# Joint buffers for the two fp16 halves of a row: one transpose of 2048 columns for two of 1024, and one load for both rotary tables

## The chip, the cores and the metric

The kernel runs on one core of one Trainium2 chip. The metric is device time in microseconds (us); the kernel before took 1997.04 us, the median of three runs. Engines are called as in the profile: PE (matmul), PEld (its weight load), DVE, ACT, POOL, and SP, which in this kernel does no arithmetic and issues every DMA, the transposes among them.

## The reference

Two layers of a hybrid encoder on a sequence of 2048 tokens of width 1024, then a final norm. Cut to what matters:

```python
def hybrid_layer(x, norm_gain, w_in, w_out, rel_bias, cos, sin):
    hn = rms_norm(x, norm_gain)
    aq, ak, av, ag, rq, rk, rv, rg = split(hn @ w_in)        # eight parts of 512 columns
    ya = chunked_rel_attention(aq, ak, av, rel_bias)         # 8 heads of 64, own chunk of 64 + 8 before
    yr = chunkwise_retention(rq, rk, rv, cos, sin)           # 4 heads of 128, rotary phases, group norm
    y = concatenate([ya * silu(ag), yr * silu(rg)])          # 2048 x 1024
    return x + y @ w_out
def reference(x, ...):
    for layer in range(2): x = hybrid_layer(x, ...)
    return rms_norm(x, final_gain)
```

## The kernel before

**Number format.** Products run on PE in fp16. Each f32 operand is split into an upper half (rounded to fp16) and a lower half (the rest, in fp16), and a product is the sum of three: upper by upper, upper by lower, lower by upper. So everything that goes to PE exists twice, as `...h` and `...l`.

**Tiling.** 128 rows of tokens are a token tile; there are 16, t = 0 to 15. Four token tiles make a stretch n of 512 tokens. A layer has four sections s, each with its share of the attention and retention heads. The normed input of a layer, turned so that the width lies on the partitions, is kept in `hTh` and `hTl`, one pair a stretch, 8 blocks of 128 rows by 512 tokens each.

**Within a section and stretch.** `dense_T` (product at L758) and `dense_V` (L778) make q, k, v and gates from `hTh`/`hTl` and the weights `whT`/`wlT`, `whV`/`wlV`. `dense_T` loads the rotary tables `tabc` and `tabs` (cosine and sine, 256 KB each, L638 and L639), which POOL multiplies into q and k of the retention (L695, L696). Attention goes unit by unit: PE makes the scores `S` (L826, L827), DVE adds the bias and takes the maximum into `sc` (L830), ACT takes the exponential in place (L833) and writes its upper half into `pq` (L835), POOL writes the lower half behind it (L836), SP turns `pq` into `pT` by one DMA transpose (L838), and PE multiplies by v (L848, L849). `sc`, `pq` and `pT` have two buffers each.

**At a layer's end** the rows of y, which sections stored to `y_d`, go through W_out, a token tile at a time. For tile t: load y (`yyy`, L959), squares on ACT (L981), a scale, the upper half on ACT (L236, `rows_hi`), the lower half on DVE (L242, `rows_lo`), and two transposes of 1024 columns on SP (L246, `transpose_rows`, called by `y_turn`) into `yhy` and `yly`; PE then does 48 matmuls of 512 columns with W_out's `whO` and `wlO` (L1115), in the order upper by upper, upper by `wlO`, lower by upper; DVE adds x; x is stored (L1123). At layer 0's end x of the tile is also normed at once for layer 1 (`residual`): squares, root, product with the gain (L1024), upper half on ACT (L236), lower half on DVE (L240), two transposes (L246) into `hTh` and `hTl` of layer 1.

**Where rows lie.** A row pair is a place for 128 rows of 1024 columns, upper and lower. At layer 0's end tiles 0 to 7 of y use room in `hTl`/`hTh` of a stretch that is not needed yet (so `yhy<-hTl` in the profile is a turn of y), the residual of tiles 0 to 3 uses the weight buffers `whT` and `wlT`, and the others take attention's `sc` (upper) and `pq` (lower): `rhy`, `rly` for y, `rhn`, `rln` for the residual. At layer 1's end all of y uses `hTh`/`hTl`. The turned y uses the buffers `tabc`, `tabs` for even t, `qq`, `swp` for odd t, `pT` for t = 15.

**What sets the order.** On PE, ACT, DVE and POOL the order is that of the program; at the layers' ends two tables of step names (`LAYER`, `LAST`) say in which round of PE's work each step stands (`yh7` is the upper half of tile 7's y, `nl4` the lower half of tile 4's residual, `nx4` its transposes, `yt7` the turn of y). SP's order is found by a scheduler, except for some DMAs that are held in the program's order. A DMA waits on SP until its sources and its target are free, and whatever stands behind it in SP's queue waits too.

Of the kernel before, what the change touches and what calls it, by code (L numbers as in the profile page):

```python
# [18 lines left out]
P = 128  # L19
# [8 lines left out]
def hybrid_trunk(ctx: ExitStack, tc: tile.TileContext, x, pos, gain, gcol, w_in, w_out, rel, fgain,  # L28
# [180 lines left out]
    hT = {}  # L209
    ring = {}  # L210
# [13 lines left out]
    def hT_of(l, n):  # L224
        if (l, n) not in hT:
            hT[l, n] = (hp.tile([P, KT, 512], F16, tag="hTh", name=f"hTh{l}_{n}"),
                        hp.tile([P, KT, 512], F16, tag="hTl", name=f"hTl{l}_{n}"))
        return hT[l, n]

    def row_pair(nm):  # L230
        return (b2.tile([P, 1280], F16, tag="sc", name=f"rh{nm}")[:, 0:D],
                b2.tile([P, 1280], F16, tag="pq", name=f"rl{nm}")[:, 0:D])

    def rows_hi(rows, xt, s_=None):

        act.activation(rows[0], xt, AF.Copy, scale=1.0 if s_ is None else s_[:, 0:1])  # L236

    def rows_lo(rows, xt, s_=None):
        if s_ is None:
            dve.tensor_tensor(rows[1], xt, rows[0], op=ALU.subtract)  # L240
        else:
            dve.scalar_tensor_tensor(out=rows[1], in0=xt, scalar=s_[:, 0:1], in1=rows[0], op0=ALU.mult, op1=ALU.subtract)  # L242

    def transpose_rows(rows, dh, dl, turn=False):
        for d, r in ((dh, rows[0]), (dl, rows[1])):
            i = sp.dma_start_transpose(out=d, in_=r)  # L246
            if turn:
                in_turn(i)

    class Tok:  # L250
# [46 lines left out]
        def dma(self):  # L297
            transpose_rows(self.rw, self.hh, self.hl)
# [330 lines left out]
    def dense_T(l, s, n, g, st):  # L629
        hh, hl = hT[l, n]  # L630
        nm = f"{l}_{s}_{n}"
        st.tabc = b1.tile([P, 512], F32, tag="tabc", name=f"tabc{nm}")
        st.tabs = b1.tile([P, 512], F32, tag="tabs", name=f"tabs{nm}")
        def tab_load():
            while n not in tab_done:
                assert bg
                pull(1)
            in_turn(sp.dma_start(st.tabc, tab_d[n][0]))  # L638
            in_turn(sp.dma_start(st.tabs, tab_d[n][1]))  # L639
# [164 lines left out]
    def attention(l, s, n, g, st, prev):  # L804
# [6 lines left out]
        def qk(a, hx):  # L811
# [16 lines left out]
            v = b2.tile([P, 640], F32, tag="sc", name=f"sc{u.nm}")[:, 0:w]  # L828
# [5 lines left out]
            pq = b2.tile([P, 1280], F16, tag="pq", name=f"pq{u.nm}")  # L834
# [139 lines left out]
    def y_squares(l, u):  # L974
        u.m = b2.tile([P, 1], F32, tag="ym", name=f"ym{u.nm}")
        if l + 1 == DEPTH or u.t < 8:
            f = (hT[l, 1] if l + 1 == DEPTH else hT_of(l + 1, NS - 2))[u.t // 2 % 2].rearrange("p k c -> p (k c)")
            u.rows = [f[:, (u.t % 2 * 2 + i) * D:(u.t % 2 * 2 + i + 1) * D] for i in range(2)]
        else:
            u.rows = row_pair(u.nm)  # L980
        act.activation(u.rows[0], u.y, AF.Square, accum_out=u.m)  # L981
# [28 lines left out]
    def residual(l, t, xt, rows):  # L1010

        hh, hl = (h_[:, :, t % 4 * P:(t % 4 + 1) * P] for h_ in hT_of(l, t // 4))
# [20 lines left out]
        for f, fn in (("q", sq), ("r", root), ("m", mul), ("u", upper), ("l", lower),  # L1033
                      ("x", lambda: transpose_rows(u.rows, hh, hl))):
# [27 lines left out]
    def wout(l, go, gc, us, wT=None):  # L1062
# [6 lines left out]
        for r in range(6 * NT):  # L1069
# [46 lines left out]
            if i % 3 == 2:  # L1116
# [59 lines left out]
    def norm_steps(ts, spaces, rows):  # L1176
# [495 lines left out]
```

## Time and profile before

| | |
|---|---|
| median of 3 runs | 1997.04 us (1996.8 to 1997.64) |
| the profiled execution: its time | 1997.53 us |
| its span, first to last instruction | 1995.8 us |
| PE busy | 1977.3 us (99%) |
| DVE, ACT, POOL busy | 1233.1, 1153.7, 699.2 us |
| granted clock of PE | 1.00 |
| DMA traffic | 316.08 MB, mean 158 GB/s |

Such rows are read thus. A timeline row has the start in us, the duration in us, the engine, the source line, the operation, output <- inputs, and in brackets how long the engine stood idle before it and what released it. SPq is SP's queue: the time that it took to issue, waits of the DMA for its sources included. In the view of a tile a row has the instructions' durations in ns as shortest, median and longest; the line "DMA to landing" has the time from the begin of the issue to the data's arrival as shortest, median and longest. In the view of waits a row has who waited, for whom, the total in us, how often, and the longest.

### The profile page before, as it was taken

How to read it: one execution, taken by the hardware profiler on the slowest of the kernel's cores; microseconds unless marked ns; L12 is line 12 of the kernel's file. 1: busy time of each engine (PE TensorE's matmuls, PEld its weight loads, DVE VectorE, ACT ScalarE, POOL GpSimd, SP SyncE). 2: the span in 40 equal slices, each digit the busy share in tenths (PEclk: the TensorE clock that was granted, in tenths of full speed). 3: DMA queues.
4: the chain of work that ended last, by engine and by line, in shares of the span. 5: the costliest groups of instructions: out<-in, count | busy, mean ns of one | idle time of the engine just before them, and what ended most of it. 6: DMA issues, size and time to landing. Idle time of an engine off the chain costs nothing.

```text
span 1995.8 us, 36717 instructions
## 1 busy us (share of the span) xinstructions
PE 1977.3 (99%) x12874; PEld 1039.7 (52%) x12874; DVE 1233.1 (62%) x3665; ACT 1153.7 (58%) x2523; POOL 699.2 (35%) x701
## 2 busy tenths in 40 slices
PE   8999999999999999999999999999999999999998
PEld 5455555555555555554445555555555555555544
DVE  8787756665556655676545556555655565567544
ACT  8667756465656545655445556565656565456432
POOL 1444343434434334420013444344333443343100
PEclk9999999999999999999999999999999999999999
DMA  8899566566655654999974556665566485568864
GB/s 248 189 189 198 145 140 145 131 141 137 143 126 145 145 121 117 217 235 265 266 161 108 105 122 136 144 146 110 138 151 150 104 180 125 122 126 190 234 200 137
DMA packets 657899, 316.08 MB, mean 158 GB/s; under 512 B 471569, under 2 KB 614417, under 8 KB 657714
## 3 DMA queue, kind: packets, MB, share of 16 engines
q1 hardware_dynamic: 657714, 313.75, 68.1%
q8 instruction: 100, 1.64, 0.4%
q14 instruction: 85, 0.70, 0.1%
HBM read 122.74 MB, written 41.98 MB: 83 GB/s over the span
## 4 chain that ended last, share of the span: by engine, by line
PE 94%; DMA 1%; DVE 1%; issue 0%; POOL 0%; ACT 0%; SPq 0%; POOLq 0%; ACTq 0%
PE dV L778 32%; PE dT L758 31%; PE dO L1115 16%; PE r L883 4%; PE o L848 3%; PE S L826 3%; PE S L827 3%; PE o L849 2%; DMA yly<-hTl 0%; DMA pT<-pq 0%; DVE hTl L1002 0%; DMA swp<-rot 0%; DVE hTh L1191 0%; DVE hTl L242 0%; POOL swp L696 0%
## 5 line engine op out<-in xcount | busy, mean ns | idle before, releaser
L836 POOL TENSOR_TENSOR pq<-sc,pq 128x640 f16<-128x640 f32 (+4 forms) x256 | 322.2, 1259 | 949.7 <-ACT pq L835 463.2
L833 ACT ACTIVATE sc<-sc,mq,cT 128x640 f32<-128x640 f32 (+4 forms) x256 | 218.3, 853 | 397.3 <-DVE mq L832 288.5
L778 PE MATMUL dV<-whV,hTh 128*128 128x512 f16 x1024 | 351.5, 379 | 0.0
L778 PE MATMUL dV<-wlV,hTh 128*128 128x512 f16 x1024 | 351.5, 379 | 0.0
L778 PE MATMUL dV<-whV,hTl 128*128 128x512 f16 x1024 | 351.5, 379 | 0.0
L758 PE MATMUL dT<-hTh,whT 128*128 128x512 f16 x992 | 340.5, 379 | 0.5 <-DVE xb L96 0.5
L758 PE MATMUL dT<-hTh,wlT 128*128 128x512 f16 x992 | 340.5, 379 | 0.0
L758 PE MATMUL dT<-hTl,whT 128*128 128x512 f16 x992 | 340.5, 379 | 0.0
L778 PEld LDWEIGHTS <-hTh 128*128 128x128 f16 x2048 | 195.9, 98 | 211.4
L758 PEld LDWEIGHTS <-whT 128*128 128x128 f16 x1984 | 189.0, 98 | 202.1 <-DVE hTl L290 1.0
L830 DVE CUSTOM_DVE_ANT_0 sc<-S,bias 128x640 f32<-128x640 f32 (+4 forms) x256 | 188.5, 736 | 134.2 <-PE S L827 133.2
L1115 PE MATMUL dO<-whO,yly 128*128 128x512 f16 x504 | 191.0, 379 | 1.9 <-DMA yly<-hTl 1.9
L1115 PE MATMUL dO<-whO,yhy 128*128 128x512 f16 x504 | 191.0, 379 | 0.0
L1115 PE MATMUL dO<-wlO,yhy 128*128 128x512 f16 x504 | 191.0, 379 | 0.0
L835 ACT ACTIVATE pq<-sc 128x640 f16<-128x640 f32 (+4 forms) x256 | 171.5, 670 | 8.1
L1115 PEld LDWEIGHTS <-yhy 128*128 128x128 f16 x1008 | 98.0, 98 | 113.7 <-issue 0.3
L778 PEld LDWEIGHTS <-hTl 128*128 128x128 f16 x1024 | 99.0, 98 | 110.1
L758 PEld LDWEIGHTS <-wlT 128*128 128x128 f16 x992 | 95.8, 98 | 106.2
L826 PE MATMUL S<-k,q 128*128 128x128 f16 (+3 forms) x592 | 142.4, 267 | 0.0
L848 PE MATMUL o<-v,pT 128*128 128x129 f16 x1120 | 132.4, 221 | 0.4 <-DMA pT<-pq 0.4
L827 PE MATMUL S<-k,q 128*128 128x128 f16 (+3 forms) x592 | 129.3, 266 | 0.0
L849 PE MATMUL o<-v,pT 128*128 128x65 f16 x1120 | 125.7, 193 | 0.0
(357 smaller groups left out, 3260.9 us busy)
## 6 DMA issues: line engine op xcount, KB each, us to landing
q<-qq SPq DMA_DIRECT2D x128, 128.0 KB, 2.4
yyy<-y_d SPq DMA_DIRECT2D x32, 512.0 KB, 4.5
stT<-in_w_in_dram SPq DMA_DIRECT2D x27, 512.0 KB, 5.0
stV<-in_w_in_dram SPq DMA_DIRECT2D x26, 512.0 KB, 4.5
k<-kk SPq DMA_DIRECT2D x128, 64.0 KB, 2.0
swp<-rot SPq DMA_DIRECT2D x64, 128.0 KB, 3.7
tabc<-tab SPq DMA_DIRECT2D x32, 256.0 KB, 2.9
tabs<-tab SPq DMA_DIRECT2D x32, 256.0 KB, 3.1
```

Source lines behind the costliest of these rows:

```text
L758: pe.matmul(ps, w_[:, j, kt, :], h_[:, kt, :], start=(m == 0), stop=(m == 23))
L778: pe.matmul(ps, h_[:, kt, a * P:(a + 1) * P], w_[:, kt, :], start=(m == 0), stop=(m == 23))
L826: pe.matmul(o, st.q[:, hx, 0, cs], k_, start=True, stop=False)
L827: pe.matmul(o, st.q[:, hx, 1, cs], k_, start=False, stop=True)
L830: dve.tensor_tensor_reduce(out=v, in0=S[:, 0:w], in1=g.bias[hx][:, 640 - w:640], scale=1.0, scalar=-3.0e38, op0=ALU.add, op1=ALU.max, accu ...
L833: act.activation(v, v, AF.Exp, bias=m[:, 0:1], scale=g.c[:, 0:1])
L835: act.activation(pq[:, 0:w], v, AF.Copy)
L836: pool.tensor_tensor(pq[:, w:2 * w], v, pq[:, 0:w], op=ALU.subtract)
L848: pe.matmul(o[:, u.hx, 0:129], u.p[:, b, :], v_, start=(b == 0), stop=False)
L849: pe.matmul(o[:, u.hx, 0:65], u.p[:, u.nb + b, :], v_[:, 0:65], start=False, stop=(b == u.nb - 1))
L883: pe.matmul(out_, w_, m_, start=(i == 0), stop=(i + 1 == len(pairs)))
L1115: pe.matmul(ps, h_[:, kt, :], w_[:, kt, :], start=(m == 0), stop=(m == 23))
```

## The change

The two halves of a row pair now lie side by side in one buffer, and so do the two halves of the turned result; where nothing else forbids it, one transpose of 2048 columns turns both.

- `hTh` and `hTl` become one tile `hT`, upper half first.
- `sc` (f32, 640 columns) and `pq` (fp16, 1280 columns) become one tile `sc` of 2560 fp16 columns with two buffers. Attention uses its first half for scores and its second for the fp16 halves. A row pair takes its first 2048 columns.
- `residual`'s transposes at layer 0's end: one of 2048 columns a tile. For t < 4 both halves lie in `wT.g.h` or both in `wT.g.l`.
- `y_turn`: even t by one transpose of 2048 columns into the tables' buffer, odd t still by two of 1024.
- The rotary tables become one tile `tab`, loaded by one DMA of 512 KB, 32 times in all.
- The transposes at layer 0's start stay in halves.

```diff
     def hT_of(l, n):
         if (l, n) not in hT:
-            hT[l, n] = (hp.tile([P, KT, 512], F16, tag="hTh", name=f"hTh{l}_{n}"),
-                        hp.tile([P, KT, 512], F16, tag="hTl", name=f"hTl{l}_{n}"))
+            both = hp.tile([P, 2, KT, 512], F16, tag="hT", name=f"hT{l}_{n}")
+            hT[l, n] = (both[:, 0], both[:, 1])
+            turned[l, n] = both.rearrange("p h k c -> p (h k) c")
         return hT[l, n]
+    def turned_of(l, t):
+        return turned[l, t // 4][:, :, t % 4 * P:(t % 4 + 1) * P]
     def row_pair(nm):
-        return (b2.tile([P, 1280], F16, tag="sc", name=f"rh{nm}")[:, 0:D],
-                b2.tile([P, 1280], F16, tag="pq", name=f"rl{nm}")[:, 0:D])
+        return b2.tile([P, 2560], F16, tag="sc", name=f"rw{nm}")[:, 0:2 * D].rearrange("p (h c) -> p h c", h=2)
...
-    def transpose_rows(rows, dh, dl, turn=False):
-        for d, r in ((dh, rows[0]), (dl, rows[1])):
-            i = sp.dma_start_transpose(out=d, in_=r)
+    def transpose_rows(rows, out):
+        sp.dma_start_transpose(out=out, in_=rows.rearrange("p h c -> p (h c)"))
+
+    def transpose_halves(rows, hi, lo, turn=False):
+        for h, d in enumerate((hi, lo)):
+            i = sp.dma_start_transpose(out=d, in_=rows[:, h])
             if turn:
                 in_turn(i)
...
-        st.tabc = b1.tile([P, 512], F32, tag="tabc", name=f"tabc{nm}")
-        st.tabs = b1.tile([P, 512], F32, tag="tabs", name=f"tabs{nm}")
+        tab = b1.tile([P, 2, 512], F32, tag="tab", name=f"tab{nm}")
+        st.tabc, st.tabs = tab[:, 0], tab[:, 1]
...
-            in_turn(sp.dma_start(st.tabc, tab_d[n][0]))
-            in_turn(sp.dma_start(st.tabs, tab_d[n][1]))
+            in_turn(sp.dma_start(tab, tab_d[n].rearrange("h p c -> p h c")))
...
-            v = b2.tile([P, 640], F32, tag="sc", name=f"sc{u.nm}")[:, 0:w]
+            both = b2.tile([P, 2560], F16, tag="sc", name=f"sc{u.nm}")
+            v, pq = both[:, 0:1280].bitcast(F32)[:, 0:w], both[:, 1280:2560]
...
-            pq = b2.tile([P, 1280], F16, tag="pq", name=f"pq{u.nm}")
...
     def y_turn(u, end=False):
+        if u.t % 2 == 0:
+            both = b1.tile([P, 2 * KT, P], F16, tag="tab", name=f"yT{u.nm}")
+            u.h, u.lo = both[:, 0:KT], both[:, KT:2 * KT]
+            transpose_rows(u.rows, both)
+            return
         if u.t + 1 == NT:
             u.h, u.lo = (b2.tile([P, 10, P], F16, tag="pT", name=f"y{c}{u.nm}")[:, 0:KT, :] for c in "hl")
         else:
-            u.h = b1.tile([P, KT, P], F16, tag=("tabc", "qq")[u.t % 2], name=f"yh{u.nm}")
-            u.lo = b1.tile([P, KT, P], F16, tag=("tabs", "swp")[u.t % 2], name=f"yl{u.nm}")
-        transpose_rows(u.rows, u.h, u.lo, end and u.t == 1)
+            u.h, u.lo = (b1.tile([P, KT, P], F16, tag=g_, name=f"y{c}{u.nm}") for c, g_ in (("h", "qq"), ("l", "swp")))
+        transpose_halves(u.rows, u.h, u.lo, end and u.t == 1)
...
-        hh, hl = (h_[:, :, t % 4 * P:(t % 4 + 1) * P] for h_ in hT_of(l, t // 4))
+        hh = hT_of(l, t // 4)[0][:, :, t % 4 * P:(t % 4 + 1) * P]
...
-                      ("x", lambda: transpose_rows(u.rows, hh, hl))):
+                      ("x", lambda: transpose_rows(u.rows, turned_of(l, t)))):
...
-                        rows = [w_[:, 2 + t % 2].rearrange("p k c -> p (k c)") for w_ in (wT.g.h, wT.g.l)]
+                        rows = (wT.g.h, wT.g.l)[t % 2][:, 2:4].rearrange("p h k c -> p h (k c)")
```

The rows of PE, ACT, DVE and POOL stand in the same order as before; their waits differ. SP has 1330 rows where it had 1394. The changed program's line numbers lie 4 to 12 higher (L246 is now L250 for a joint transpose and L254 for a half, L830 is L839, L838 is L846).

**SP at layer 0's end, the turning of y of tiles 6 and 7.** `hT...<-whT` and `<-wlT` are the residual of tile 3, `<-rhn_4` and `<-rln_4` that of tile 4, `x_d` and `y_d` are stores, `yyy` a load of y; a wait names the engine or the DMA queue waited for. Before:

```order
L246 DMA_TRANSPOSE hTh_0_11428<-whT_0_11279 128x8x128 [waits DMAHW2_49,Activation_49]
L246 DMA_TRANSPOSE yhy_6_12128<-hTl_2_10626 128x8x128 [waits DMAHW3_49,PE_49,Activation_49]
L1123 DMA x_d_125<-hTh_3_10628 128x1024 [waits DMAHW4_49,DVE_49]
L864 DMA y_d_120<-ya_3_3_3_1_12051 128x128 [waits DMAHW5_49]
L246 DMA_TRANSPOSE yly_6_12129<-hTl_2_10626 128x8x128 [waits DMAHW6_49,PE_49]
L246 DMA_TRANSPOSE hTl_0_11429<-wlT_0_11280 128x8x128 [waits DMAHW7_49,DVE_49]
L246 DMA_TRANSPOSE hTh_1_12079<-rhn_4_12172 128x8x128 [waits DMAHW0_49,Activation_49]
L246 DMA_TRANSPOSE yhy_7_12227<-hTl_2_10626 128x8x128 [waits DMAHW1_49,PE_49]
L1123 DMA x_d_126<-hTh_3_10628 128x1024 [waits DMAHW2_49,DVE_49]
L959 DMA yyy_9_12186<-y_d_114 128x1024 [waits DMAHW3_49]
L246 DMA_TRANSPOSE hTl_1_12080<-rln_4_12173 128x8x128 [waits DMAHW4_49,DVE_49]
L246 DMA_TRANSPOSE yly_7_12228<-hTl_2_10626 128x8x128 [waits DMAHW5_49,PE_49]
```

Now:

```order
L250 DMA_TRANSPOSE yTy_6_11951<-hT_2_10477 128x16x128 [waits DMAHW4_49,DVE_49,PE_49]
L1135 DMA x_d_125<-hT_3_10479 128x1024 [waits DMAHW5_49,DVE_49]
L872 DMA y_d_120<-ya_3_3_3_1_11875 128x128 [waits DMAHW6_49]
L250 DMA_TRANSPOSE hT_0_11266<-wlT_0_11120 128x16x128 [waits DMAHW7_49,DVE_49]
L254 DMA_TRANSPOSE yhy_7_12044<-hT_2_10477 128x8x128 [waits DMAHW0_49,PE_49,Activation_49]
L1135 DMA x_d_126<-hT_3_10479 128x1024 [waits DMAHW1_49,DVE_49]
L967 DMA yyy_9_12005<-y_d_114 128x1024 [waits DMAHW2_49]
L250 DMA_TRANSPOSE hT_1_11903<-rwn_4_11992 128x16x128 [waits DMAHW3_49,DVE_49]
L254 DMA_TRANSPOSE yly_7_12045<-hT_2_10477 128x8x128 [waits DMAHW4_49,PE_49]
```

The turn of tile 6 stands once, where its upper half stood, and waits for DVE; the whole of tile 4's residual stands where its lower half stood, ahead of tile 7's lower half.

**SP, tile 10's turn.** `stV` are weight loads; `rhn_7`, `rwn_7` belong to the residual of tile 7. Before:

```order
L317 DMA stV_00_1_12651<-in_w_in_dram 128x4x128 [waits DMAHW2_49,DVE_49]
L246 DMA_TRANSPOSE yhy_10_12550<-rhy_10_12482 128x8x128 [waits DMAHW3_49,PE_49,Activation_49]
L1123 DMA x_d_129<-hTh_3_10628 128x1024 [waits DMAHW4_49,DVE_49]
L959 DMA yyy_12_12534<-y_d_117 128x1024 [waits DMAHW5_49,DVE_49]
L246 DMA_TRANSPOSE yly_10_12551<-rly_10_12483 128x8x128 [waits DMAHW6_49,PE_49]
L246 DMA_TRANSPOSE hTh_1_12079<-rhn_7_12538 128x8x128 [waits DMAHW7_49,Activation_49]
L246 DMA_TRANSPOSE hTl_1_12080<-rln_7_12539 128x8x128 [waits DMAHW0_49,DVE_49]
```

Now:

```order
L325 DMA stV_00_1_12453<-in_w_in_dram 128x4x128 [waits DMAHW6_49,DVE_49]
L1135 DMA x_d_129<-hT_3_10479 128x1024 [waits DMAHW7_49,DVE_49]
L967 DMA yyy_12_12343<-y_d_117 128x1024 [waits DMAHW0_49,DVE_49]
L250 DMA_TRANSPOSE yTy_10_12358<-rwy_10_12292 128x16x128 [waits DMAHW1_49,PE_49]
L250 DMA_TRANSPOSE hT_1_11903<-rwn_7_12347 128x16x128 [waits DMAHW2_49,DVE_49]
```

The joint turn stands where the lower half's stood; nothing of tile 10 goes out ahead of the store and the load.

**DVE, an attention unit of layer 0.** The row of L830 (L839 now) is bias and maximum; the rows around it belong to the unit before and to the retention. Before:

```order
L862 TENSOR_TENSOR ya_3_2_0_1_10852<-o_3_2_0_0_10766,gt_3_2_0_10298 128x128 [waits DVE_49]
L923 SCALAR_TENSOR_TENSOR state_3_0_9476<-r_3_9_10900,state_3_0_9476 128x128 [waits PE_49,Activation_49]
L830 ISA sc_3_2_2_0_10943,mq_3_2_2_0_10944<-S_3_2_2_0_10936,bias_6_8794 128x640 [waits PE_49]
L830 ISA mq_3_2_2_0_10944 128x1
L832 TENSOR_SCALAR mq_3_2_2_0_10944<-mq_3_2_2_0_10944,ncT_3_6935 128x1 [waits DVE_49]
```

Now:

```order
L870 TENSOR_TENSOR ya_3_2_0_1_10699<-o_3_2_0_0_10614,gt_3_2_0_10155 128x128 [waits DVE_49]
L931 SCALAR_TENSOR_TENSOR state_3_0_9347<-r_3_9_10746,state_3_0_9347 128x128 [waits PE_49,Activation_49]
L839 ISA sc_3_2_2_0_10789,mq_3_2_2_0_10790<-S_3_2_2_0_10782,bias_6_8674 128x640 [waits DMAHW7_49,PE_49]
L839 ISA mq_3_2_2_0_10790 128x1
L841 TENSOR_SCALAR mq_3_2_2_0_10790<-mq_3_2_2_0_10790,ncT_3_6842 128x1 [waits DVE_49]
```

DVE's row now waits for a DMA queue as well: that of the transpose which reads the buffer two units earlier. Before, ACT's copy (L835) had that wait.

More of the change, by code (lines that the diff above doesn't have):

```diff
@@ L209, in hybrid_trunk @@
     hT = {}
+    turned = {}
     ring = {}
@@ L977, in y_squares @@
             f = (hT[l, 1] if l + 1 == DEPTH else hT_of(l + 1, NS - 2))[u.t // 2 % 2].rearrange("p k c -> p (k c)")
[L978 removed]
+            u.rows = f[:, u.t % 2 * 2 * D:(u.t % 2 + 1) * 2 * D].rearrange("p (h c) -> p h c", h=2)
         else:
             u.rows = row_pair(u.nm)
[L981 removed]
+        act.activation(u.rows[:, 0], u.y, AF.Square, accum_out=u.m)
     def y_scale(u, go):
```

19 lines of the change are left out of this document (10 added, 9 removed).

## The prediction

> **What bounds the kernel now.** I read the page's first and fourth parts, then PE's own waits, then PE's and SP's rows at the layer's end.
>
> ```profile
> PE 1977.3 (99%) x12874; PEld 1039.7 (52%) x12874; DVE 1233.1 (62%) x3665; ACT 1153.7 (58%) x2523; POOL 699.2 (35%) x701
> PE 94%; DMA 1%; DVE 1%; issue 0%; POOL 0%; ACT 0%; SPq 0%; POOLq 0%; ACTq 0%
> ```
>
> PE is busy 1977.3 of 1995.8 us, and the chain that ended last is PE for 94%. The change takes no matmul away, so it can gain only where PE stands still. PE's waits:
>
> ```profile
> PE ptn L276 <- DVE ssn L219: 3.2, 1, 3.2
> PE msg L340 <- DVE mbg L333: 2.9, 1, 2.9
> PE dO L1115 <- DMA yly<-hTl: 1.9, 2, 1.2
> PE msh L340 <- DMA gb<-in_gain_dram: 1.8, 1, 1.8
> ```
>
> The large ones (3.2, 2.9, 1.8) are single waits on the input's norm and gains, before the first layer's work, where the transposes stay in halves. What the change can reach is the third line: twice W_out's matmuls waited for a turned lower half of y. How much time that was is read from PE's starts:
>
> ```profile
> 902.23 0.38 PE L1115 MATMUL dO<-wlO,yhy 128*128 128x512 f16 x1
> 903.24 0.39 PE L1115 MATMUL dO<-whO,yly 128*128 128x512 f16 x1 [0.64 <-DMA yly<-hTl]
> ...
> 913.42 0.38 PE L1115 MATMUL dO<-wlO,yhy 128*128 128x512 f16 x1
> 915.04 0.39 PE L1115 MATMUL dO<-whO,yly 128*128 128x512 f16 x1 [1.24 <-DMA yly<-hTl]
> ...
> 1896.06 0.38 PE L1115 MATMUL dO<-whO,yly 128*128 128x512 f16 x1
> 1896.71 0.38 PE L1115 MATMUL dO<-whO,yly 128*128 128x512 f16 x1
> ```
>
> The last two rows lie three matmuls apart: 0.65 / 3 = 0.217 us a matmul, so a token tile's 48 take 10.4 us. Against that, tile 6 lost 1.01 - 0.22 = 0.8 us and tile 7 lost 1.62 - 0.22 = 1.4: 2.2 us at layer 0's end. That is 0.11% of the run, and it is the most that a perfect outcome brings. A measurement of this kernel tells about 0.2%, 4.0 us, from no change. So the question is only whether new waits arise. Where:
>
> ```profile
> 900.00:940.00 40.00, 38.12 (x180) 17.04 (x179) 28.32 (x70) 23.68 (x41) 1.86 (x4) 1.00 1.11 263
> 1900.00:1990.00 90.00, 89.74 (x440) 41.87 (x438) 40.15 (x81) 24.17 (x37) 5.64 (x9) 1.00 0.60 174
> ```
>
> The columns are the stretch, busy us of PE, PEld, DVE, ACT, POOL, then PE's clock (1.00), the DMA share and GB/s. At layer 0's end (the first row) the 16 DMA engines are full (1.11); at layer 1's end (the second) they are at 0.60.
>
> **The change part by part.** *What one transpose of 2048 columns costs* is in no row; two shapes bound it.
>
> ```profile
> L838 SPq DMA_TRANSPOSE pT<-pq x256: 1168/1337/4084, 71.1 to 1865.2; - x128
> DMA to landing us min/median/max: 2.3/3.0/6.7
> ...
> L710 SPq DMA_TRANSPOSE kt<-rot x32: 1232/1259/2543, 72.4 to 1814.8; - x32
> DMA to landing us min/median/max: 3.1/3.2/4.9
> ```
>
> The first is attention's (256 to 1280 columns, mostly 1280), the second has 1024. SP's issue grows from 1.17 us (the shortest) to 1.34 (1280): 0.165 ns a column, so about 1.46 for 2048, against 2 x 1.26 = 2.52 for two halves. The landing goes from 2.3 to 3.0 over 1024 columns, so 2048 would land 3.0 + 0.5 = 3.5 us after its issue begins; were it no better than two halves in a row, at 1.26 + 3.2 = 4.5. I take 4.0: a joint transpose whose halves are both ready lands 0 to 1 us before the pair's second half did. The moved bytes are the same.
>
> [...] The full stretch above moved 263 GB/s, plain loads included.
>
> *SP* loses 64 of 1394 issues: 32 table loads, 16 transposes of the residual, 16 of y. That is 32 x (2.52 - 1.46) = 34 us, and 32 x 0.39 (row below) = 12, of an engine that is not on the path; it counts only where SP is late.
>
> *The rotary tables.* Tightest is the first pair:
>
> ```profile
> 45.68 0.53 SPq L638 DMA_DIRECT2D tabc<-tab  x1
> 46.31 0.39 SPq L639 DMA_DIRECT2D tabs<-tab  x1
> 48.60 1.52 POOL L695 TENSOR_TENSOR rot<-rot,tabc 128x512 f32<-128x512 f32 x1 [2.77 <-DMA tabc<-tab]
> ...
> 51.43 2.13 POOL L697 TENSOR_TENSOR rot<-rot,swp 128x512 f32<-128x512 f32 x1
> 55.41 0.54 SPq L691 DMA_DIRECT2D swp<-raw  x1
> ```
>
> POOL starts as the first table lands, 2.9 us after its issue; one load of 512 KB lets it start 0.6 us later (where the second table lands, 46.31 + 2.9) to 1.5 (an allowance of half of 2.9 for the doubled bytes). POOL's product ends at 53.56 and the next user comes at 55.41, 1.85 later: cost 0. Were that cover gone, 1.5 us, once.
>
> *Attention's joint buffer.* Bias and maximum on DVE (L830) of unit i now write into a buffer that the transpose of unit i-2 reads; before, only ACT's copy (L835) and POOL waited for it. The tightest place:
>
> ```profile
> 797.47 1.75 SPq L838 DMA_TRANSPOSE pT<-pq  x1
> 805.44 0.82 DVE L830 CUSTOM_DVE_ANT_0 sc<-S,bias 128x640 f32<-128x640 f32 x1 [2.40 <-PE S L827]
> ```
>
> That transpose cannot have landed later than the run's longest, 6.7 us: 804.17, which is 1.27 before DVE starts, and DVE waits there for PE. Behind DVE's wait would stand ACT's exponential and PE's next product. Cost 0; if the cover failed, the excess over 1.27 at that unit.
>
> *y at layer 1's end:* even tiles lose the head start of the upper half.
>
> ```profile
> 1885.93 1.25 SPq L246 DMA_TRANSPOSE yhy<-hTl  x1
> 1888.13 1.23 SPq L246 DMA_TRANSPOSE yly<-hTl  x1
> ```
>
> A joint one goes out where the lower did, at 1888.13, lands at 1892.1 to 1892.6, and PE needs the lower half at 1896.71: 4 us of cover, cost 0.
>
> *y and the residual at layer 0's end*, where a term is left:
>
> ```profile
> 894.70 3.50 SPq L246 DMA_TRANSPOSE yhy<-hTl  x1
> ...
> 899.39 1.74 SPq L246 DMA_TRANSPOSE yly<-hTl  x1
> ...
> 902.61 1.30 SPq L246 DMA_TRANSPOSE hTh<-rhn  x1
> ...
> 906.47 1.82 SPq L246 DMA_TRANSPOSE hTl<-rln  x1
> 908.38 3.04 SPq L246 DMA_TRANSPOSE yly<-hTl  x1
> ...
> 892.00 1.28 DVE L242 SCALAR_TENSOR_TENSOR hTl<-yyy,sy,hTl 128x1024 f16<-128x1024 f32 x1 [0.58 <-ACT hTl L236]
> ...
> 904.80 1.22 DVE L240 TENSOR_TENSOR rln<-xnn,rhn 128x1024 f16<-128x1024 f32 x1
> ...
> DMA to landing us min/median/max: 6.6/6.6/6.6
> ```
>
> Tile 6 (even): its lower half was ready at 893.28, yet its transpose went out at 899.39, behind the upper half and two stores. The joint one goes in the upper half's place, by about 895, and even with 5.5 us to land it is there at 900.5, before PE's 902.4. The 0.8 us go. At worst, if the full DMA engines hold it 2.3 us more, they stay.
>
> Tile 7 (odd, in halves) stands in SP's queue behind the residual of tile 4, whose joint transpose now waits for DVE until 904.80 + 1.22 = 906.02. After its 1.46 tile 7's lower half goes out near 907.6 instead of 908.38, but behind 1024 more columns, which before had gone at 902.61 and cost 0.5 to 1.0 us of landing. With the 6.6 us of the last row (the tile's view: the landing of the transpose issued at 908.38) it lands at 914.7 to 915.2, as before (914.98). Cost 0; ends: -1.4 (it vanishes) and +1.6 (a full 1.3 us transpose ahead of it, a little more).
>
> Tile 10 (even) had nothing to spare:
>
> ```profile
> 936.29 2.33 SPq L246 DMA_TRANSPOSE yhy<-rhy  x1
> ...
> 939.80 2.43 SPq L246 DMA_TRANSPOSE yly<-rly  x1
> ...
> 946.18 0.38 PE L1115 MATMUL dO<-whO,yly 128*128 128x512 f16 x1
> ...
> 942.92 1.06 ACT L981 ACTIVATE rhy<-yyy 128x1024 f16<-128x1024 f32 x1 [2.40 <-DMA yhy<-rhy]
> ...
> DMA to landing us min/median/max: 6.2/6.2/6.2
> ```
>
> Its lower half landed at 939.80 + 6.2 = 946.0 (the last row, again the tile's view), and PE took it at 946.18. Joint, it carries the upper half too, so 0 to 1.3 us later (1.3: the issue of a half), but SP is free of 936.29's issue and may begin 1.5 earlier. I take +0.2, ends 0 and 1.1. The ACT row is the next user of that row buffer, tile 11's squares: it waited for the upper half alone, until 942.92, and now waits until 946.0 or so, 3.1 us more. What that does to tile 11 is mostly repaid by the two transposes that SP no longer issues ahead of its own (2 x 1.06): +0.1, ends 0 and 2.0.
>
> Sum: -0.8 + 0 + 0.2 + 0.1 = -0.5 us. The profiled execution took 1997.53 us (span 1995.8 and 1.7 around it), 0.5 above the median of 1997.04; so 1997.0 for it, and 1996.5 for the median. The ends are -0.8 - 1.4 = -2.2 and 0 + 1.6 + 1.1 + 2.0 = +4.7.
>
> **The rivals.** *The row buffers become the loop* (other side). Two buffers serve y and the residual, and ACT already waits for them. If the 3.1 us by which tile 10's buffer comes free later recur, each tile pays 3.1 - 2.4 (ACT's idle time) = 0.7 us, or half of 3.1, 1.6, if that idle time is part of the loop and only even tiles pay. Over tiles 10 to 15 this is 4.2 to 9.6; less 0.8 it gives 2000.4 to 2005.8, in the middle 2003. It decides once a joint transpose lands after PE's need, 946.2 at tile 10, and the next tiles do not win it back. For it: the 0.2 us of margin and the full DMA engines. Against it: SP issues less, and later tiles wait less. [...]
>
> *All stalls of the layer's end go*: 1997.04 - 2.2 = 1994.8. For it: 64 fewer issues on SP, which stood behind tiles 6 and 7. Against it: tile 7 is not turned jointly, and waits behind one that is.
>
> *It is hidden or merely moves the stalls*: tile 6's 0.8 comes back at tiles 7, 10 and 11, and the time is 1997.0 to 1998.5. For it: no order changes on PE, ACT, DVE and POOL.
>
> **How the numbers follow.** Likeliest, 1996.5 (within 1995.5 to 1997.0): 0.47. Hidden or moved: 0.24. All stalls gone: 0.14. The row-buffer loop: 0.13, of which 0.11 lies beyond +4.0 us. Something that no row shows and that gains over 4 us: 0.02. No sign holds against 0.2% but in the last two, so faster 0.02, same 0.87, slower 0.11. The range takes the three middle cases and the loop's low end: 1994.5 (0.3 below the case of no stalls, about what the lowest run lies below the median, 0.24) to 2001.0.
>
> **What would show it.** Right: 64 fewer SP rows; no wait of PE at tile 6; one of about 1.4 us at tile 7; a joint transpose that issues in about 1.46 us and lands after 3.5 to 4.5 where DMA is not full; no wait of PE elsewhere that was not there. Wrong: waits of PE for turned y at tile 10 and after, or ACT's waits for row buffers growing by 3 us a tile; a joint issue of 2.5 us; DVE's L839 waiting for a transpose.

## The result, and the profile after

The changed kernel takes 2004.51 us (median of 6 runs, 2003.92 to 2005.03) against 1997.43 us: 7.1 us slower, ratio 1.0035 with an interval of 1.0022 to 1.0048. The forecast was 1996.5 us, with a range of 1994.5 to 2001.0. (One later run of the kernel before took 4807.14 us and is left out of what follows.) The changed kernel's page (busy time, and the chain that ended last):

```profile
PE 1978.6 (99%) x12874; PEld 1039.0 (52%) x12874; DVE 1233.3 (62%) x3665; ACT 1154.6 (58%) x2523; POOL 703.3 (35%) x701
PE 90%; DMA 4%; ACT 2%; SPq 1%; DVE 1%; issue 1%; POOL 1%; POOLq 0%; ACTq 0%; DVEq 0%
```

No engine has noticeably more work (POOL's 4 us are the most); PE's share of the chain fell from 94% to 90%, and those of DMA and ACT rose from 1% and 0% to 4% and 2%. Where PE lost the time is read from the busy time of two stretches, the kernel before first and the changed one behind it (columns as in the prediction):

```profile
0.00:110.00 110.00, 99.51 (x655) 55.35 (x656) 89.95 (x220) 81.72 (x166) 35.35 (x51) 1.00 0.88 222
880.00:1015.00 135.00, 133.08 (x643) 60.71 (x641) 87.37 (x196) 68.76 (x121) 9.78 (x14) 1.00 1.07 259
```

```profile
0.00:110.00 110.00, 98.72 (x650) 54.83 (x651) 88.78 (x218) 81.04 (x164) 35.45 (x51) 1.00 0.86 220
880.00:1015.00 135.00, 128.79 (x619) 58.02 (x618) 82.62 (x190) 67.41 (x114) 8.88 (x13) 1.00 1.05 250
```

PE stood idle for 1.9 us at layer 0's end before, and for 6.2 after; 0.8 us more went in the first 110 us. (An idle time in brackets is about 0.16 us short of the loss, since a matmul's modelled 0.38 us overlaps the next one, 0.22 later. With eight pauses after and two before, layer 0's end lost 5.3 us more and the start about 1, of a span that grew by 6.7.) What PE waited for there, by the changed kernel's view of waits from 880 to 1015 us:

```profile
PE dO L1127 <- DVE hT L1130: 1.6, 2, 1.1
PE msT L348 <- DVE mbT L341: 1.5, 1, 1.5
PE msV L348 <- DVE mbV L341: 1.4, 1, 1.4
PE dO L1127 <- DMA yly<-hT: 1.2, 2, 0.6
PE dO L1127 <- DMA yTy<-rwy: 0.3, 1, 0.3
```

Only the last two lines (and one of 0.2, left out) are waits for turned rows of y. Three quarters of the idle time, 4.5 of 6.2 us, is PE waiting for DVE: for the emptying of W_out's PSUM (L1130), and for the column maxima of the next layer's weights (L341), which have nothing to do with the transposes. (In a second profiled execution of the same kernel, e16 below, it is 5.0 of 8.2 us.) One of these pauses, followed back (timelines of SP, ACT, DVE and PE of the changed kernel):

```profile
953.71 2.83 SPq L250 DMA_TRANSPOSE hT<-rwn  x1
...
958.20 1.06 ACT L989 ACTIVATE rwy<-yyy 128x1024 f16<-128x1024 f32 x1 [5.84 <-DMA hT<-rwn]
...
959.38 0.15 DVE L992 TENSOR_SCALAR ymy<-ymy 128x1 f32<-128x1 f32 x1 [4.95 <-ACT rwy L989]
...
960.14 0.74 DVE L1130 SCALAR_TENSOR_TENSOR hT<-dO,oscy,hT 128x512 f32<-128x512 f32 x1
...
960.93 0.38 PE L1127 MATMUL dO<-whO,yhy 128*128 128x512 f16 x1 [1.10 <-DVE hT L1130]
```

The residual of tile 8 is turned jointly from 953.71 and lands at about 958.1. Until then its row buffer is held, and ACT waits 5.84 us to write the squares of tile 12 into it. DVE's next instruction takes the sum of these squares, so DVE stands for 4.95 us; behind it in DVE's order stands the emptying of a PSUM bank that PE needs, and PE stops for 1.10 us (the last experiment shows what else was late there). The pause at 1009 has the same form, with the residual of tile 13 waiting for that of tile 11:

```profile
1004.28 1.02 ACT L240 ACTIVATE rwn<-xnn 128x1024 f16<-128x1024 f32 x1 [3.90 <-DMA hT<-rwn]
1005.34 1.23 DVE L244 TENSOR_TENSOR rwn<-xnn,rwn 128x1024 f16<-128x1024 f32 x1 [1.84 <-ACT rwn L240]
...
1009.10 0.16 PE L348 MATMUL msV<-mbV,ones 128*128 128x1 bf16 x1 [1.39 <-DVE mbV L341]
```

These are ACT's waits for row buffers, from its view of waits from 880 to 1015 us, the kernel before first:

```profile
ACT rhn L236 <- DMA hTh<-rhn: 6.5, 2, 4.1
ACT rhn L236 <- DMA yhy<-rhy: 4.8, 2, 3.5
ACT rhy L981 <- DMA hTh<-rhn: 3.5, 1, 3.5
```

```profile
ACT rwn L240 <- DMA yTy<-rwy: 11.4, 3, 4.6
ACT rwy L989 <- DMA hT<-rwn: 10.8, 2, 5.8
ACT rwn L240 <- DMA hT<-rwn: 8.2, 3, 3.9
ACT rwy L989 <- DMA yTy<-rwy: 6.0, 1, 6.0
ACT rwy L989 <- DMA yly<-rwy: 2.5, 1, 2.5
```

With the 2.4 us of tile 11 that the prediction shows, ACT waited 17.2 us for row buffers before, always for an upper half; now it waits 38.9 us, for the landing of both. Part of this only changed engines: the lower halves' buffers had made DVE wait 6.0 us before, and DVE no longer waits for any.

### The profile page after: what moved, and what is told of

It reads as the page before. It is cut to its first block, busy times and chain, and to the rows that moved or that the text cites. A ratio compares the mean times of both kernels' runs of the same rounds, so it can differ in the third digit from the quotient of the medians.

```text
span 2002.5 us, 36662 instructions
## 1 busy us (share of the span) xinstructions
PE 1978.6 (99%) x12874; PEld 1039.0 (52%) x12874; DVE 1233.3 (62%) x3665; ACT 1154.6 (58%) x2523; POOL 703.3 (35%) x701
## 4 chain that ended last, share of the span: by engine, by line
PE 90%; DMA 4%; ACT 2%; SPq 1%; DVE 1%; issue 1%; POOL 1%; POOLq 0%; ACTq 0%; DVEq 0%
PE dV L786 31%; PE dT L766 31%; PE dO L1127 14%; PE r L891 4%; PE o L856 3%; PE S L834 3%; PE S L835 3%; PE o L857 2%; DMA hT<-rwn 1%; DMA yTy<-rwy 1%; DMA hT<-in_x_dram 1%; DMA pT<-sc 0%; DMA yly<-hT 0%; DMA xa<-in_x_dram 0%; SPq L1403 0%
## 5 line engine op out<-in xcount | busy, mean ns | idle before, releaser
L844 POOL TENSOR_TENSOR sc<-sc 128x640 f16<-128x640 f32 (+4 forms) x256 | 323.2, 1262 | 952.0 <-ACT sc L843 459.3
L786 PE MATMUL dV<-whV,hT 128*128 128x512 f16 x2048 | 577.8, 379 | 0.3 <-DVE gt L804 0.3
L766 PE MATMUL dT<-hT,whT 128*128 128x512 f16 x1984 | 564.6, 379 | 0.5 <-DVE xb L96 0.5
L786 PEld LDWEIGHTS <-hT 128*128 128x128 f16 x3072 | 292.2, 98 | 322.3 <-DVE gt L804 0.8
L786 PE MATMUL dV<-wlV,hT 128*128 128x512 f16 x1024 | 351.5, 379 | 0.0
L766 PE MATMUL dT<-hT,wlT 128*128 128x512 f16 x992 | 340.5, 379 | 0.0
L839 DVE CUSTOM_DVE_ANT_0 sc<-S,bias 128x640 f32<-128x640 f32 (+4 forms) x256 | 188.6, 737 | 136.7 <-PE S L835 135.9
L843 ACT ACTIVATE sc<-sc 128x640 f16<-128x640 f32 (+4 forms) x256 | 171.5, 670 | 8.1
L1127 PE MATMUL dO<-whO,yTy 128*128 128x512 f16 x512 | 155.2, 379 | 0.8 <-DVE hT L1130 0.5
L835 PE MATMUL S<-k,q 128*128 128x128 f16 (+3 forms) x592 | 129.3, 266 | 0.0
L856 PEld LDWEIGHTS <-pT 128*128 128x128 f16 x1120 | 103.4, 97 | 32.1 <-DMA pT<-sc 2.2
L857 PEld LDWEIGHTS <-pT 128*128 128x128 f16 x1120 | 101.0, 99 | 29.9
L950 POOL TENSOR_TENSOR rss<-rss,mhalf 128x1 f32<-128x1 f32 x128 | 95.0, 742 | 11.0 <-DVE rss L949 9.0
```

The costliest lines, as they stand in the source:

```text
L766: pe.matmul(ps, w_[:, j, kt, :], h_[:, kt, :], start=(m == 0), stop=(m == 23))
L786: pe.matmul(ps, h_[:, kt, a * P:(a + 1) * P], w_[:, kt, :], start=(m == 0), stop=(m == 23))
L835: pe.matmul(o, st.q[:, hx, 1, cs], k_, start=False, stop=True)
L839: dve.tensor_tensor_reduce(out=v, in0=S[:, 0:w], in1=g.bias[hx][:, 640 - w:640], scale=1.0, scalar=-3.0e38, op0=ALU.add, op1=ALU.max, accu ...
L843: act.activation(pq[:, 0:w], v, AF.Copy)
L844: pool.tensor_tensor(pq[:, w:2 * w], v, pq[:, 0:w], op=ALU.subtract)
```

## The experiments

The theory after the comparison: **row buffers**. A joint buffer comes free only when both halves have landed; ACT waits for that, DVE stands behind ACT and PE behind DVE. Its rivals: **SP's queue** (a joint transpose waits on SP for DVE's lower half and holds what stands behind), and the other joint things (input tile, tables, attention). Times are medians; "over" is against the kernel before as measured beside it (1998.06 us for e1 to e4, 1997.89 for e5 to e8, 1997.77 for e9 to e12, 1997.96 for e13 to e16, 1997.28 for e17); the last column is 135 us less PE's busy time from 880 to 1015 us, in the one profiled execution (1.9 before, 6.2 in the changed kernel). Another execution of the changed kernel (e16) has 8.2 there, so a difference of 2 us in this column alone decides nothing.

| kernel | us | over | ratio, interval | PE idle |
|---|---|---|---|---|
| e1 residual in halves | 2004.14 | +6.1 | 1.0033, 1.0020 to 1.0045 | 6.5 |
| e2 y in halves | 2004.42 | +6.4 | 1.0032, 1.0019 to 1.0044 | 6.8 |
| e3 all in halves | 2002.83 | +4.8 | 1.0022, 1.0013 to 1.0032 | 4.6 |
| e4 y's rows to tile 10 elsewhere | 2005.45 | +7.4 | 1.0037, 1.0024 to 1.0049 | 7.9 |
| e5 tables only | 1998.35 | +0.5 | 1.0002, 0.9993 to 1.0011 | 2.4 |
| e6 input tile only | 1997.80 | -0.1 | 0.9998, 0.9990 to 1.0007 | 2.4 |
| e7 attention's buffer only | 2000.93 | +3.0 | 1.0015, 1.0006 to 1.0024 | 2.9 |
| e8 two table loads | 2006.89 | +9.0 | 1.0043, 1.0030 to 1.0055 | 9.6 |
| e9 as e7, residual's own buffers | 2002.39 | +4.6 | 1.0021, 1.0013 to 1.0030 | 4.5 |
| e10 as e1, residual's own buffers | 2001.96 | +4.2 | 1.0021, 1.0012 to 1.0030 | 3.5 |
| e11 odd y's own buffers | 2005.81 | +8.0 | 1.0040, 1.0028 to 1.0053 | 7.3 |
| e12 before, residual's own buffers | 2000.00 | +2.2 | 1.0010, 1.0001 to 1.0018 | 2.7 |
| e13 as e9, SP's order held | 1999.06 | +1.1 | 1.0003, 0.9994 to 1.0012 | 1.7 |
| e14 as e10, SP's order held | 2000.68 | +2.7 | 1.0013, 1.0004 to 1.0022 | 2.5 |
| e15 as e12, SP's order held | 1997.76 | -0.2 | 0.9999, 0.9990 to 1.0008 | 1.0 |
| e16 the changed kernel again | 2005.20 | +7.2 | 1.0035, 1.0022 to 1.0047 | 8.2 |
| e17 the changed kernel, one DVE instruction moved | 2005.88 | +8.6 | 1.0036, 1.0022 to 1.0050 | 8.4 |

**First: take the joint transposes back, or move rows of y.** Edits to the changed kernel (e1 the first, e2 the second, e3 both, e4 the third):

```diff
-                      ("x", lambda: transpose_rows(u.rows, turned_of(l, t)))):
+                      ("x", lambda: transpose_halves(u.rows, hh, hl))):
...
-            transpose_rows(u.rows, both)          # y_turn, even t
+            transpose_halves(u.rows, u.h, u.lo)
...
-        if l + 1 == DEPTH or u.t < 8:             # y_squares: rows in the input tile
+        if l + 1 == DEPTH or u.t < 11:
```

> The changed kernel, but the residual's transposes at layer 0's end go out in halves again (16 pairs); y's even tiles stay joint, buffers stay joint. Three theories for the 7 us. Row buffers: a row buffer comes free only when both halves have landed, ACT waits for it, DVE stands behind ACT and PE behind DVE; halves in a joint buffer are freed by the later half as well, so most of the loss stays: 2001 to 2004 us. SP's queue: a joint transpose waits on SP until DVE has written the lower half and holds up whatever stands behind it (tile 5's and tile 7's halves of y behind the residual); then this one recovers most of it: 1998.5 to 2000. Start: what was lost by tile 4 (about 1 us, tables and attention) stays in both.

> The changed kernel, but y's even tiles are turned in halves again (into the joint tables' buffer); the residual stays joint. Row buffers: as the residual's experiment, 2001 to 2004 us. SP's queue: the residual's joint transposes are the ones that stand ahead of others, so little comes back: 2002.5 to 2004.5.

> The changed kernel with joint buffers and joint table loads, but every transpose at the layers' ends in halves. Row buffers: a joint buffer is still held until the second half has landed, so 2001 to 2003 us. SP's queue: all but the start's 1 us comes back: 1997.5 to 1999.

> The changed kernel with all its joint transposes, but the rows of y of tiles 8, 9 and 10 lie where those of tiles 4 to 6 lay (in the tile of a stretch of layer 1 that is not yet needed) and not in attention's buffers, so that y and the residual share the two row buffers only from tile 11 on. Row buffers: the waits of ACT before tiles 9 to 11 go, and with them PE's stalls between 930 and 960 us (about 4 us): 1999.5 to 2001.5. SP's queue: no transposes are moved or split, so 2003.5 to 2005.

With every transpose in halves (e3) 4.8 of the 7 us stay: the joint transposes are not the main cause, as the row buffers had it, and SP's queue as the main cause falls (it expected 1997.5 to 1999). e1 and e2 alone cannot be told from the changed kernel. e4 missed: nothing came back. Its timelines of ACT, SP and PE show why:

```profile
953.16 1.02 ACT L240 ACTIVATE rwn<-xnn 128x1024 f16<-128x1024 f32 x1 [8.19 <-DMA hT<-rwn]
...
941.72 6.74 SPq L250 DMA_TRANSPOSE yTy<-hT  x1
...
951.46 0.39 PE L1127 MATMUL dO<-whO,yTy 128*128 128x512 f16 x1 [2.45 <-DMA yTy<-hT]
```

As soon as tile 11 entered the two buffers, the residual of tile 8 had to wait for that of tile 7, 8.19 us: the edit had moved ACT's wait, not taken it away. And PE's longest pause there, 2.45 us, was for the joint turn of tile 10, whose rows lie in no row buffer in e4; it held SP for 6.74 us. So e4 does not decide for or against the row buffers, and it shows a joint turn that is late though its rows lie outside them.

**Second: one joint thing at a time**, on the kernel before (e5 tables with one load, e6 input tile, e7 the diff below), and e8: the changed kernel with the tables loaded by two DMAs into the joint tile.

```diff
-        return (b2.tile([P, 1280], F16, tag="sc", name=f"rh{nm}")[:, 0:D],
-                b2.tile([P, 1280], F16, tag="pq", name=f"rl{nm}")[:, 0:D])
+        rw = b2.tile([P, 2560], F16, tag="sc", name=f"rw{nm}")
+        return rw[:, 0:D], rw[:, D:2 * D]
...                                                # and v, pq in one tile "sc" in attention
```

> The kernel before with one thing of the change: the joint tables' tile and its one load of 512 KB (y's even tiles use it, in halves). The trace of the changed kernel has POOL's first product with the tables 1.1 us later and PE's pauses 0.5 us larger at 59 and 0.7 at 101. If this load is the cause, +1.0 to 1.5 us over before; if that loss comes from the joint input tile or attention's joint buffer, 0 to +0.3.

> The kernel before with one thing of the change: the joint input tile (both halves of a stretch in one tile, still two transposes each). Theory of the row buffers (attention's joint buffer, held by a row pair until the later half has landed): the input tile is not involved, 0 to +0.5 us. Rival: rows of y and of x lie in that tile at the layer's end, and a joint tile widens their waits: +2 to +4.

> The kernel before with one thing of the change: attention's scores and fp16 halves, and the row pairs, in one joint buffer; all transposes in halves. Theory of the row buffers: most of what the form with all transposes in halves still lost, +2.5 to +4 us, with ACT waiting for the later half before tiles 9 to 12. Rival (input tile): 0 to +1.

> The changed kernel, with the two tables loaded by two DMAs of 256 KB into the joint tile. If the joint load costs at the start, 1.0 to 1.5 us come back (2003 us beside the changed kernel's 2004.5); if not, 2004 to 2005.

Only attention's joint buffer is slower by itself, by 3.0 us (2.5 to 4 expected), though all its transposes are in halves. ACT's waits in e7 show the same release as in the changed kernel, 37.1 us in all, now for the lower half:

```profile
ACT rwn L236 <- DMA yly<-rwy: 11.7, 4, 3.7
ACT rwy L981 <- DMA yly<-rwy: 10.3, 2, 6.4
ACT rwy L981 <- DMA hTl<-rwn: 8.5, 2, 5.2
ACT rwn L236 <- DMA hTl<-rwn: 6.6, 2, 5.5
```

The input tile costs nothing that can be measured. The tables are at +0.5 with an interval that holds no change. e8 removed PE's pause at 59 us, but was not faster than the changed kernel; its layer end lost more (9.6 us idle). The changed kernel's own two executions differ there by 2 us, so a gain of 0.5 to 1 us at the start is not visible behind it.

**Third: take the residual out of the shared buffers.** Its rows of tiles 4 to 15 go where attention's biases and k lie, three buffers of each (e9 on e7, e10 on e1, e12 on the kernel before); e11 moves the odd tiles of y in the same way and keeps all joint transposes.

```diff
-            u.rows = rows or row_pair(nm)
+            u.rows = rows or (b3.tile([P, 1280], F16, tag="bias", name=f"nh{nm}")[:, 0:D],
+                              b3.tile([P, D], F16, tag="k", name=f"nl{nm}"))
```

> As the kernel with only attention's joint buffer (which took 2000.9 us, 3.0 over before), but the residual's rows of tiles 4 to 15 lie in other buffers (upper half where biases lie, lower half where k lies, three of each), so that only y uses the two joint ones. Row buffers: the 3.0 us go, 1997.5 to 1998.8. Rival (the joint buffer costs within attention, by its wider wait): 2000 to 2001.5.

> The changed kernel with the residual in halves (2004.1 us), and its rows of tiles 4 to 15 in buffers of their own as above; y's even tiles stay joint. Row buffers: what was lost from 930 to 1010 us (about 5 us) goes, 1998.5 to 2000.5. Rival (joint transposes of y themselves, through SP and the full DMA engines): 2002.5 to 2004.5.

> The changed kernel with all its joint transposes, but the rows of odd tiles of y (9, 11, 13, 15) lie in the biases' and k's buffers; even tiles and the residual share the two joint ones. Row buffers: about half of the waits of ACT go, and 2 to 4 us come back: 2000.5 to 2002.5. SP's queue (joint transposes wait for DVE and hold what is behind): 2003.5 to 2005.

> The kernel before, with the residual's rows of tiles 4 to 15 in buffers of their own. Row buffers: ACT's 17 us of waits for them go, but PE waited for none of these: 1996.5 to 1998, the two waits of tiles 6 and 7 stay.

The times missed: e9 was not faster than e7, and even the kernel before lost 2.2 us (e12). The timelines of e12 (SP, then PE) show a new pause:

```profile
962.14 1.24 SPq L246 DMA_TRANSPOSE hTh<-nhn  x1
963.49 1.28 SPq L246 DMA_TRANSPOSE yhy<-rhy  x1
...
969.05 0.39 PE L1116 MATMUL dO<-whO,yly 128*128 128x512 f16 x1 [1.85 <-DMA yly<-rly]
```

With other buffers the scheduler had put the upper half of residual 9 ahead of tile 12's turn on SP. It waited for ACT until 962, and tile 12 with it. PE's pauses between 930 and 960, which e7 and e1 have, were gone in e9 and e10 (the kernel before and e12 have none there), but the new one hid that in the time. In e11 even tiles and the residual still waited for each other (9.9 and 6.9 us in ACT's waits).

**Fourth: the same with SP's order held.** e13, e14 and e15 are e9, e10 and e12 with residual 9's transposes kept in the program's order:

```diff
-                      ("x", lambda: transpose_rows(u.rows, hh, hl))):
+                      ("x", lambda: transpose_rows(u.rows, hh, hl, t == 9))):
```

> As the earlier kernel with attention's joint buffer alone and the residual's rows in buffers of their own (2002.4 us), with the residual's transposes of tile 9 held in the program's order. There PE's stalls from 930 to 960 were gone, and a new one of 2.3 us at 968 came from SP: the scheduler had put residual 9's upper half ahead of tile 12's turn. Row buffers: with that mended, 1997.5 to 1999. Rival (the joint buffer costs elsewhere): 2000 to 2002.

> As the changed kernel with the residual in halves and its rows in buffers of their own (2002.0 us), with the residual's transposes of tile 9 held in the program's order. Row buffers: 1998.5 to 2000.5, against 2004 with the shared joint buffers. Rival (joint turns of y): 2001.5 to 2003.5.

> The kernel before with the residual's rows in buffers of their own (2000.0 us) and the residual's transposes of tile 9 in the program's order: the stall of 2.0 us at 967 goes, 1997 to 1998, no better than before by more than 1 us, since only tiles 6 and 7 made PE wait there.

> The changed kernel itself on the same chip as these three: 2004 to 2005.5 us, 6.5 to 7.5 over before.

PE's busy time from 880 to 1015 us in e7 and e13, and behind them in e1 and e14:

```profile
880.00:1015.00 135.00, 132.12 (x634) 59.54 (x633) 86.12 (x197) 68.06 (x115) 8.89 (x13) 1.00 1.07 255
...
880.00:1015.00 135.00, 133.34 (x643) 60.63 (x642) 87.73 (x196) 68.71 (x121) 9.78 (x14) 1.00 1.07 259
```

```profile
880.00:1015.00 135.00, 128.53 (x618) 57.82 (x615) 82.20 (x190) 67.10 (x113) 8.87 (x13) 1.00 1.07 251
...
880.00:1015.00 135.00, 132.54 (x639) 60.14 (x637) 86.84 (x201) 68.26 (x115) 9.20 (x14) 1.00 1.11 257
```

With the joint buffer and no shared residual (e13) the loss falls from 3.0 to 1.1 us, no longer distinct from none; in the changed kernel with the residual in halves (e14) it falls from 6.1 to 2.7, and PE's idle time from 6.5 to 2.5. ACT's views of e13 and e14 hold no wait for a row buffer any more. So the row buffers carry some 2 of the 3.0 us, and 3.4 of the 6.1, by the medians; the intervals of each pair still touch (1.0006 to 1.0024 and 0.9994 to 1.0012; 1.0020 to 1.0045 and 1.0004 to 1.0022). The single runs hardly overlap: all 11 of e13 (1996.67 to 1999.89 us) lie below all 11 of e7 (2000.04 to 2002.10), with the kernel before at 1997.96 and 1997.89 beside them, and 10 of the 11 of e14 lie below all five of e1. The kernel before gains nothing from the same move (e15), as expected: its ACT waits were covered. So what e13 and e14 won back belongs to the joint buffers that y and the residual shared. e13 and e14 ended 0.1 and 0.2 above the ranges expected for the row buffers, and below the rivals'. No version was measurably faster than the kernel before.

**Fifth: move one DVE instruction past the waiting one.** In the table of steps, tile 12's scale (`yc12`) and upper half come a round or two later, which puts one PSUM emptying of tile 10 ahead of the sums on DVE and changes no other engine's order:

```diff
-             ("Bin0 yl13", "yc12"), ("nx8", "nq9 yh12"), ("", ""),
+             ("Bin0 yl13", ""), ("nx8", "nq9"), ("yc12", "yh12"),
```

> The changed kernel with one DVE instruction moved: the emptying of W_out's PSUM of tile 10's first half (L1130) now stands ahead of tile 12's scale, which waits for ACT's squares and so for a row buffer; SP's, ACT's and PE's orders are the same. If DVE's order is what carries ACT's wait to PE, the pause at 961 us (1.10 us in the changed kernel's trace, 1.27 by starts) goes, ACT's wait of 5.8 us before tile 12 stays, and the time is 0.5 to 1.5 us under the changed kernel's: 2003 to 2004.5. If PE waited there for something else, the pause stays and the time is 2004.5 to 2005.5.

The timelines of e17 (DVE, then PE):

```profile
957.88 0.75 DVE L1130 SCALAR_TENSOR_TENSOR hT<-dO,oscy,hT 128x512 f32<-128x512 f32 x1 [0.36 <-DMA hT<-in_x_dram]
963.16 0.15 DVE L992 TENSOR_SCALAR ymy<-ymy 128x1 f32<-128x1 f32 x1 [4.53 <-ACT rwy L989]
...
964.72 0.39 PE L1127 MATMUL dO<-whO,yly 128*128 128x512 f16 x1 [1.37 <-DMA yly<-rwy]
```

PE's wait of 1.10 us for the PSUM went, so DVE's order had carried it. But the time did not fall: PE now waits 1.37 us, two matmuls later, for the lower half of tile 11. In the changed kernel that half went out at 957.26 and landed 4.0 us later, at 961.3, hidden by the pause that ended at 960.93. By the rows, both go back to tile 11's squares, which had waited 6.02 us for tile 10's joint transpose. So where two things are late from one cause, the releaser that the profile names is only the later of the two.

What stays open: e14's remaining 2.7 us (1.0004 to 1.0022). Its trace has the start's pauses and 2.05 us at tile 7 among them, but no run separates them. Nor does one separate the lateness of tile 10's joint turn (the failed step, below) from the row buffers: PE's wait for it was 0.30 us in the changed kernel's first execution, 1.73 in the second, 2.45 in e4 and 2.96 in e11, and 0.17 or less where the residual goes in halves (e1, e10, e14).

## Why the prediction was wrong, point by point

**What bounds the kernel** held: the change could gain only at layer 0's end, and the question was which new waits arise.

**The price of a joint transpose** was a little low where the DMA engines are not full, and far too low where they are. At layer 1's end (share 0.61 from 1900 to 1990 us, and 0.81 in the 4.6 us of the one shown) the changed kernel's tile view has for one of the quickest:

```profile
L250 SPq DMA_TRANSPOSE yTy<-hT x1: 1672/1672/1672, 1884.2 to 1884.2; - x1
DMA to landing us min/median/max: 4.6/4.6/4.6
```

That is 1.67 us to issue for 1.46, and 4.6 to land for 3.5 to 4.5. At layer 0's end, with the engines full (share 1.09 in the 7.8 us of each), the turns of tiles 6 and 10 took 5.79 and 4.87 us to issue and landed after 7.8 us each. PE waited nowhere at layer 1's end, as forecast.

**Tile 6** came out right by luck: its 0.8 us are gone, but its joint turn landed at 902.8, not at 900.5, after PE's old start on the tile (902.0); PE lost nothing because it came 2.2 us later itself. **Tile 7** kept 0.57 us in brackets, 0.7 by starts, of its 1.4, inside its ends; that is luck in part too, since its lower half landed at 915.8, not at 914.7 to 915.2, and PE came 1.4 us later. **Tile 5** was not priced at all, and became a pause of 1.1 us:

```profile
886.69 2.96 SPq L250 DMA_TRANSPOSE hT<-whT  x1
889.75 1.24 SPq L254 DMA_TRANSPOSE yhy<-hT  x1
...
894.25 0.39 PE L1127 MATMUL dO<-whO,yly 128*128 128x512 f16 x1 [0.59 <-DMA yly<-hT]
```

The joint transpose of tile 2's residual held SP for 2.96 us ahead of tile 5's halves. That it is the cause is likely, not shown: with the residual in halves 0 to 0.23 us were left (e1, e3, e14), but e6 and e9, without any joint transpose, had 0.55 and 0.96 us there. The prediction named this for tile 7 and did not look for other places of the same pattern.

**Tile 10, and what hangs on it, is the step that failed.** The term for tile 10 itself (+0.2, ends 0 and 1.1) fits PE's 0.30 us in brackets by luck only. The turn was to begin up to 1.5 us before 939.80, when the lower half had gone out, and to land near PE's need at 946.2. It began at 940.82, after DVE had written the lower half at 940.35, and landed at 948.6. PE hardly waited because it came 2.4 us later itself; in the second execution (e16) it waited 1.73 us. For tile 11, the step that called the buffer's lateness "mostly repaid by the two transposes that SP no longer issues" was wrong:

```profile
939.07 1.28 DVE L246 SCALAR_TENSOR_TENSOR rwy<-yyy,sy,rwy 128x1024 f16<-128x1024 f32 x1
...
940.82 4.87 SPq L250 DMA_TRANSPOSE yTy<-rwy  x1
DMA to landing us min/median/max: 7.8/7.8/7.8
...
948.64 1.06 ACT L989 ACTIVATE rwy<-yyy 128x1024 f16<-128x1024 f32 x1 [6.02 <-DMA yTy<-rwy]
```

With full DMA engines (share 1.09 from 940.8 to 948.6) SP gained nothing here: the joint transpose held it for 4.87 us, with its rows ready since 940.35, as long as both halves had (2.33 and 2.43). The buffer came free at 948.6, where 946.0 was forecast and 942.9 was the time before; and this recurred for the pairs that followed. So tile 11's y came late after all (e17: 1.37 us, forecast 0.1, ends 0 and 2.0). And the step did not ask what stands behind the waiting ACT instruction: DVE's sums and lower halves, and behind these on DVE the emptying of PSUM and the weights' maxima, where the profile of the changed kernel has 4.5 of PE's 6.2 us. In the trace DVE kept to its order: it stood idle for 4.95 us with the emptying of PE's PSUM waiting behind.

**The rival of the row buffers** named the cause that the runs bear out for about half of the loss (3.4 of 6.1 us from e1 to e14, the rest open), but it had 0.13 of the chance. Its size fits (2000.4 to 2005.8 us, measured 2004.5) by luck: it was priced as lateness of y alone, and 4.5 of PE's 6.2 us were waits for DVE. Its main reason here is one that the prediction had not seen clearly: not the joint transpose but the joint buffer delays the release, as e7 showed with every transpose in halves (37.1 us of ACT's waits for row buffers, 17.2 before).

**The tables' cover was named wrongly.** POOL began its product 1.1 us later, inside the 0.6 to 1.5 forecast:

```profile
49.69 1.27 POOL L703 TENSOR_TENSOR rot<-rot,tab 128x512 f32<-128x512 f32 x1 [4.00 <-DMA tab<-tab]
...
59.55 0.61 PE L786 MATMUL dV<-whV,hT 128*128 128x512 f16 x2 [0.35 <-DVE gt L804]
```

The 1.85 us of cover were those of the next user of the product. POOL's own queue went on with the bias, which ACT and then DVE waited for, and PE paused at 59.55. It is 0.5 us by PE's starts; e5 measured +0.5 for the tables, no surer than that.

**Attention's wider wait** cost nothing in the changed kernel's trace: DVE waits for no transpose at L839 (135.9 us there for PE's scores, 0.4 for no engine).

## What to carry to other kernels

Two tiles that were made one were also released as one (ACT's waits for row buffers at layer 0's end: 17.2 us before, 37.1 in e7): before joining buffers, ask which half was waited for, by whom, and how late the other lands. An engine that waited cost what stood behind it in its order, not what it was about to write (DVE's 4.95 us held PE up for 1.10, through the emptying of a PSUM bank), so follow the queue of every engine in the chain to the next instruction that the bounding engine needs. A late transfer did not show where PE was late itself (tile 6's turn landed 0.8 us after PE's old start, and PE lost nothing), so compare landings, and not only waits, with a forecast. When an experiment frees a resource and the time does not fall, look first whether the wait has moved, or whether the scheduler's order has changed with it.

## What the hardware showed that was not expected

A pause of PE cost more than itself in three cases. In e9 PE stopped for 2.13 us and then ran ten matmuls at half speed:

```profile
970.43 0.39 PE L1116 MATMUL dO<-whO,yly 128*128 128x512 f16 x1 [2.13 <-DMA yly<-rwy]
...
971.36 0.63 PE L1116 MATMUL dO<-whO,yly 128*128 128x512 f16 x1
971.78 0.63 PE L1116 MATMUL dO<-whO,yhy 128*128 128x512 f16 x1
...
970.50:974.20 3.70, 3.70 (x10) 1.36 (x11) 0.52 (x4) 1.15 (x2) 0.30 (x1) 0.54 1.05 258
```

Starts lie 0.42 us apart instead of 0.22, and the granted clock of these 3.7 us (the seventh figure of the last row, from the view of windows) is 0.54: about 1.7 us more on top of the pause, an estimate from that clock (3.7 x 0.46). In e11 the same followed pauses of 2.96 and 2.19 us (clock 0.56 and 0.51). It did not follow a pause of 2.45 us in e4, whose next 4 us ran at 1.00. The changed kernel's own profile has no such stretch. The three slow stretches lasted about 3.7, 3.6 and 3.3 us. No run shows why they followed these three pauses and not the one of 2.45 us.
